# First adaLN vector of a hybrid attention block: its scale part moved to TensorE, its low halves to VectorE, its transfers rebuffered

## The chip, the cores and the metric

The kernel runs on one core of a Trainium2 chip. The metric is the device time of one execution, in microseconds (us). A core has TensorE (PE, whose weight loads are shown apart as PEld), VectorE (DVE), ScalarE (ACT), GpSimd (POOL), and SyncE (SP), whose queue issues the transfers. Each engine works through its own instructions in the order in which they stand; a program orders them when the kernel is built.

## The reference, cut to what matters

```python
ada = (c @ w_ada + b_ada)[:, None, :]            # c: 1 x 1024, w_ada: 1024 x 6144
shift1, scale1, gate1, shift2, scale2, gate2 = jnp.split(ada, 6, axis=-1)
h = rmsnorm(x, g_norm1) * (1.0 + scale1) + shift1     # x: 1024 tokens x 1024
proj = h @ w_in
(q_f, k_f, v_f, f_logit, q_d, k_d, v_d, q_i, k_i, w_i, gate_fox, gate_dsa) = jnp.split(proj, ...)
...
sc = einsum('bqhd,bkd->bqhk', q_idx, k_idx) * idx_scale        # the indexer, 4 heads
iscore = einsum('bqhk,bqh->bqk', relu(sc), w_idx)              # top 256 keys of a query
...
x = x + gate1 * (merged @ w_out)
h2 = rmsnorm(x, g_norm2) * (1.0 + scale2) + shift2
x = x + gate2 * (square(relu(h2 @ w_mlp1)) @ w_mlp2)
return rmsnorm(x, g_final)
```

The change lies in the first two lines for `scale1` and `shift1`, in `h`, and in the loading of the columns of `w_in` for `q_i`, `k_i`, `w_i` and `f_logit`. Two attention branches, the merge and the MLP follow and are not edited.

## The kernel before

The first stage makes `h`, transposed: the 1024 features lie in eight blocks of 128 partitions (index `k`), the tokens along the row in two halves of 512 (index `g`). Products are made in pieces: every operand is split into a high half, rounded to the type fp32r, and a low half, the rest; each product of two such pairs takes three matmuls of 128x512 (`mm3`, hi·hi, lo·hi, hi·lo; all recorded at L75).

Eight tiles `xn` hold x, 128 tokens each; they are normalized in place (L214). The adaLN part goes block by block along `KBS`: blocks 0 and 1 alone, then 2-3, 4-5, 6-7. For each, `load_ada` brings the 1024 rows of `w_ada` for the scale (`j == 1`) and for the shift (`j == 0`) into a tile `wa` (four buffers). In both cases VectorE multiplies the eight row groups by the values of c in `cT` and sums them in `acc` (L245, L247: eight chained instructions), and a matmul with a column of ones sums over the partitions (`ada_cols`, tile `pv`), one column for a block of 128 features. Only for the scale of blocks 0 and 1 TensorE does the sum itself, with the vector c as weights and `wa` streaming. The sums go to `ab` (L175; the scale also L178, L179).

Then TensorE transposes four `xn` pieces into `xT` (two PSUM buffers), ScalarE makes `hf` from it with scale and shift (L267) and the high half `h_hi` (L268), and GpSimd the low half `h_lo` (L270). In the last pair, VectorE does all three for `g == 1`. As soon as a block of `h` is there, the six groups of products of the indexer take it: `S` twice (keys and the small columns), `g` twice, `S` and `tr` (queries), 24 matmuls each. Their weights (`whi`, `wlo`, `qi_w`) are split by ScalarE and GpSimd (L117, L118) from staging tiles `st` (three buffers).

Behind the stage stand, on VectorE, the copies of the indexer's operands (`misc`, `KAi`, `QAi`, `QBi`), and on TensorE first the scores `S<-KAi,QAi` and then the projections `g<-h_hi,whi` of the attention heads. The order on each engine is set when the program is built, by a scheduler that interleaves this code with what follows it; it is therefore different in many places after an edit, and within `tc.high_priority()` the adaLN part goes first.

Of the kernel before, what the change touches and what calls it, by code (L numbers as in the profile page):

```python
# [9 lines left out]
F32 = mybir.dt.float32  # L10
# [47 lines left out]
def block_kernel(ctx: ExitStack, tc: tile.TileContext, x, c, w_ada, b_ada, g_norm1, w_in, b_forget,  # L58
# [15 lines left out]
    def mm(o, l, r, start, stop):  # L74
        nc.tensor.matmul(o, l, r, start=start, stop=stop)  # L75
# [39 lines left out]
    def split_st(st, lo_eng=None, dst=None):  # L115
        hi, lo = dst or [wts.tile([P, 1024], F32R, name=n, tag=n) for n in ("whi", "wlo")]
        nc.scalar.activation(hi, st, AF.Copy)  # L117
        (lo_eng or nc.vector).tensor_tensor(lo, st, hi.bitcast(F32), op=ALU.subtract)  # L118
        return hi, lo
# [58 lines left out]
        nc.vector.tensor_scalar(dst, dst, 1.0, None, op0=ALU.add)  # L178
        nc.vector.tensor_tensor(dst, dst, vecT[:, g0:g0 + n], op=ALU.mult)  # L179

    def misc_weights():
        st = stg.tile([P, 1024], F32, name="st", tag="st")
        sv = st.rearrange("p (k c) -> p k c", k=KT)
        nc.gpsimd.memset(st, 0.0)
        nc.sync.dma_start(sv[:, :, 0:64], win[:, :, C_KI:C_KI + 64])
        nc.sync.dma_start(sv[:, :, 64:72], win[:, :, C_F:C_F + NH])
        nc.sync.dma_start(sv[:, :, 96:100], win[:, :, C_WI:C_WI + NIH])
        return split_st(st, nc.gpsimd)

    wav = w_ada.rearrange("(k p) n -> p k n", p=P)  # L190
    with ExitStack() as st1:
        p1 = pool(st1, "p1")
        sqj = p1.tile([P, D], BF16, name="sqj")
        xn = [p1.tile([P, D], F32, name=f"xn{t}") for t in range(NTT)]
        ss = p1.tile([P, NTT], F32, name="ss")
        nc.scalar.activation(ss[:, 0:1], onesf[:, 0:1], AF.Sqrt)
        def load_x(ts_):
            for t in ts_:
                nc.sync.dma_start(xn[t], xr[t * P:(t + 1) * P, :])

        def load_ada(kt0, n):
            was = []
            for j in (1, 0):
                wt = p1.tile([P, KT, 256], F32, name="wa", tag="wa", bufs=4)[:, :, 0:n * P]
                nc.sync.dma_start(wt, wav[:, :, j * D + kt0 * P:j * D + (kt0 + n) * P])
                was.append((j, wt))
            return was

        def norm_x(g):
            for t in range(4 * g, 4 * g + 4):  # L210
                nc.scalar.activation(sqj, xn[t], AF.Square, accum_out=ss[:, t:t + 1])
            r = newton_rstd(p1, ss[:, 4 * g:4 * g + 4], 4, f"a{g}")
            for t in range(4 * g, 4 * g + 4):
                nc.vector.tensor_scalar(xn[t], xn[t], r[:, t - 4 * g:t - 4 * g + 1], None, op0=ALU.mult)  # L214

        load_x(range(4))
        nc.sync.dma_start(vecs[0:8, :], c.rearrange("o (k p) -> (o k) p", p=P))
        nc.sync.dma_start(vecs[8:16, :], g_norm1.rearrange("(k p) -> k p", p=P))
        nc.sync.dma_start(vecs[16:24, :], g_norm2.rearrange("(k p) -> k p", p=P))
        nc.sync.dma_start(vecs[24:72, :], b_ada.rearrange("(k p) -> k p", p=P))  # L220
        vps = ptr.tile([P, 512], F32, name="vps", tag="tr")
        nc.tensor.transpose(vps[:, 0:P], vecs, ident)
        nc.vector.tensor_copy(vecT, vps[:, 0:P])
        KBS = ((0, 1), (1, 1), (2, 2), (4, 2), (6, 2))
        was = load_ada(*KBS[0])
        load_x(range(4, 8))
        norm_x(0)
        nc.sync.dma_start(bfg[64:64 + NH, :], b_forget.rearrange("(h o) -> h o", o=1))
        first = [misc_weights(), split_w([(0, P, win[:, :, C_QI:C_QI + P])], nc.gpsimd)]
        with tc.high_priority():  # L230
            for kb, (kt0, n) in enumerate(KBS):
                if kb:
                    was = load_ada(kt0, n)
                for j, wt in was:
                    acc = p1.tile([P, 256], F32, name="acc", tag=f"acc{j}")[:, 0:n * P]
                    if j == 1 and kb < 2:
                        ps = ppv.tile([P, 512], F32, name="pv", tag="pv")
                        for k in range(KT):
                            mm(ps[0:1, 0:n * P], cT[:, k:k + 1], wt[:, k, :], k == 0, k == KT - 1)
                        nc.vector.tensor_copy(acc[0:1, :], ps[0:1, 0:n * P])  # L240
                        ada_cols(acc, j, kt0, n, ab[:, 1 - j, :], ppv.tile([P, 512], F32, name="pv", tag="pv"), 1)
                    else:
                        for k in range(KT):
                            if k == 0:
                                nc.vector.tensor_scalar(acc, wt[:, k, :], cT[:, 0:1], None, op0=ALU.mult)  # L245
                            else:
                                nc.vector.scalar_tensor_tensor(acc, wt[:, k, :], cT[:, k:k + 1], acc, op0=ALU.mult, op1=ALU.add)  # L247
                        ada_cols(acc, j, kt0, n, ab[:, 1 - j, :], ppv.tile([P, 512], F32, name="pv", tag="pv"))
                if kb == 0:
                    norm_x(1)  # L250
                if kb == len(KBS) - 1:
                    first.append(split_w([(0, P, win[:, :, C_QI + P:C_QI + 2 * P])], nc.gpsimd,
                                         dst=(qi_w[:, 0:1024], qi_w[:, 1024:2048])))
                norm_scale(ab[:, 0, kt0:kt0 + n], 8 + kt0, n)
                for k in range(kt0, kt0 + n):
                    for g in range(2):
                        gs = slice(g * 512, (g + 1) * 512)
                        ps = ptr.tile([P, 512], F32, name="xT", tag="tr")
                        for t in range(4):
                            nc.tensor.transpose(ps[:, t * P:(t + 1) * P], xn[4 * g + t][:, k * P:(k + 1) * P], ident)  # L260
                        hf = p1.tile([P, 512], F32, name="hf", tag="hf", bufs=4)
                        if kb == len(KBS) - 1 and g == 1:
                            nc.vector.tensor_scalar(hf, ps, ab[:, 0, k:k + 1], ab[:, 1, k:k + 1], op0=ALU.mult, op1=ALU.add)
                            nc.vector.tensor_copy(h_hi[:, k, gs], hf)
                            lo_eng = nc.vector
                        else:
                            nc.scalar.activation(hf, ps, AF.Identity, scale=ab[:, 0, k:k + 1], bias=ab[:, 1, k:k + 1])  # L267
                            nc.scalar.activation(h_hi[:, k, gs], hf, AF.Copy)  # L268
                            lo_eng = nc.gpsimd
                        lo_eng.tensor_tensor(h_lo[:, k, gs], hf, h_hi[:, k, gs].bitcast(F32), op=ALU.subtract)  # L270

    def gemm_h(hi, lo, half, pl=None):
        pl, tag = pl or (pg, "g")
# [929 lines left out]
```

## Time and profile before

| | us |
|---|---|
| median of 3 runs (1656.96 to 1659.05) | 1657.38 |
| the profiled execution's own time | 1664.09 |
| span of the profiled execution | 1662.3 |
| TensorE busy (95% of the span) | 1582.9 |
| VectorE busy (70%) | 1155.4 |
| ScalarE busy (57%) | 955.7 |
| GpSimd busy (41%) | 684.4 |

The profiled execution is 6.7 us above the median, and 1.8 us of its time lie around the span. Busy matmul time counts overlapping pieces, so 95% doesn't mean that TensorE is at its peak.

### The profile page before, as it was taken

The page shows a single profiled execution, that of the slowest core. Times are in us where ns is not written, and L with a number is a line of the kernel's source. Part 1 is how long each engine was busy: PE and PEld are TensorE (multiplying, and loading weights), DVE is VectorE, ACT ScalarE, POOL GpSimd, SP SyncE. Part 2 cuts the span into 40 slices and gives each one's busy share as a digit, 9 for nine tenths or more (in the row PEclk, how much of TensorE's full clock was granted, in tenths as well). Part 3 has the DMA queues.
Part 4 walks back from the last instruction along what each step waited for, and adds up shares of the span by engine and source line. Part 5 has one row for each costly group of instructions (what it writes and reads, how often), then busy time and mean ns, then how long its engine had stood idle before and what let it go on. Part 6 is the DMA issues. An engine that isn't in the chain of part 4 may idle for free.

```text
span 1662.3 us, 22793 instructions
## 1 busy us (share of the span) xinstructions
PE 1582.9 (95%) x7585; PEld 1310.5 (79%) x7585; DVE 1155.4 (70%) x2293; ACT 955.7 (57%) x1674; POOL 684.4 (41%) x569
## 2 busy tenths in 40 slices
PE   5989999998989999999999998999999989999998
PEld 3767787786778888888887787888888868888887
DVE  6786999999954556556666535866565464758987
ACT  4366997898566777677753135554555343533433
POOL 3421121221123574756643211677776544334730
PEclk8999999998999999999999999999999989999999
DMA  9221122222232443444876435554444469665862
GB/s 299 77 59 51 50 74 55 52 66 49 74 77 67 125 133 106 131 143 139 287 257 230 151 121 194 168 185 160 154 147 158 178 240 361 230 212 188 281 209 102
DMA packets 221757, 250.92 MB, mean 151 GB/s; under 512 B 49072, under 2 KB 134144, under 8 KB 221640
## 3 DMA queue, kind: packets, MB, share of 16 engines
q1 hardware_dynamic: 215304, 235.83, 44.8%
q10 hardware_dynamic: 6336, 13.63, 2.1%
q8 instruction: 60, 0.98, 0.2%
q14 instruction: 57, 0.47, 0.1%
HBM read 184.38 MB, written 65.03 MB: 150 GB/s over the span
## 4 chain that ended last, share of the span: by engine, by line
PE 74%; DVE 14%; ACT 4%; DMA 4%; issue 3%; POOL 1%; SPq 1%; DVEq 0%; ACTq 0%; POOLq 0%
PE g L75 33%; PE S L75 23%; PE tr L75 8%; PE pv L75 7%; DVE bjunk L487 3%; PE ptr L572 2%; DVE acc L247 1%; DMA gt<-G_d 1%; DVE pl L574 1%; DVE sp L552 1%; DMA wap<-in_w_ada_dram 1%; ACT eqt L484 1%; ACT sp L556 1%; DVE gt L777 1%; ACT sp L559 1%
## 5 line engine op out<-in xcount | busy, mean ns | idle before, releaser
L75 PE MATMUL g<-h_hi,whi 128*128 128x512 f32 x656 | 266.5, 406 | 8.8 <-DVE KA L314 6.4
L75 PE MATMUL g<-h_hi,wlo 128*128 128x512 f32 x656 | 263.9, 402 | 0.0
L75 PE MATMUL g<-h_lo,whi 128*128 128x512 f32 x656 | 263.0, 401 | 0.0
L118 POOL TENSOR_TENSOR wlo<-st,whi 128x1024 fp32r<-128x1024 f32 x56 | 137.3, 2453 | 293.9 <-ACT whi L117 265.4
L1026 DVE TENSOR_TENSOR ut<-rw,ut 128x1024 fp32r<-128x1024 f32 x112 | 179.0, 1644 | 69.5 <-ACT ut L1025 69.5
L1025 ACT ACTIVATE ut<-rw 128x1024 fp32r<-128x1024 f32 x112 | 112.0, 1052 | 144.9 <-PE pv L75 66.5
L1040 POOL TENSOR_TENSOR rw<-rw 128x1024 f32<-128x1024 f32 x40 | 115.6, 2893 | 127.3 <-DMA rw<-in_w_mlp_dram 110.0
L75 PEld LDWEIGHTS g<-h_hi,whi 128*128 128x128 f32 x656 | 126.2, 192 | 34.8 <-DVE KA L314 4.3
L75 PEld LDWEIGHTS g<-h_hi,wlo 128*128 128x128 f32 x656 | 125.6, 191 | 24.7
L75 PEld LDWEIGHTS g<-h_lo,whi 128*128 128x128 f32 x656 | 125.8, 192 | 23.6
L75 PE MATMUL S<-ut 128*128 128x512 f32 (+1 forms) x576 | 138.2, 384 | 0.0
L75 PEld LDWEIGHTS S<-ut 128*128 128x128 f32 x576 | 106.5, 190 | 21.5 <-DVE ut L1026 0.4
L574 DVE TENSOR_TENSOR pl<-ptr,ph 128x512 fp32r<-128x512 f32 (+1 forms) x160 | 99.5, 630 | 27.2 <-ACT ph L573 23.5
L573 ACT ACTIVATE ph<-ptr 128x512 fp32r<-128x512 f32 (+1 forms) x160 | 86.1, 551 | 55.4 <-PE ptr L572 51.2
L556 ACT ACTIVATE sp<-sp,mn 128x128 f32<-128x128 f32 (+7 forms) x128 | 98.5, 771 | 28.3 <-DVE mn L552 28.1
L117 ACT ACTIVATE whi<-st 128x1024 fp32r<-128x1024 f32 x70 | 73.8, 1054 | 65.9 <-PE g L75 23.1
L487 DVE TENSOR_SCALAR_CACHE_REDUCE bjunk<-sel_all,cand 128x384 bf16<-128x384 int16 (+7 forms) x132 | 106.3, 806 | 1.4
L559 ACT ACTIVATE sp<-sp,mn 128x128 f32<-128x128 f32 (+7 forms) x128 | 96.8, 770 | 17.2 <-DVE mn L558 16.7
L75 PE MATMUL g<-ut 128*128 128x512 f32 (+1 forms) x384 | 94.7, 382 | 6.1 <-ACT ut L1025 4.6
L572 PE MATMUL ptr<-ident,sp 128*128 128x128 f32 x576 | 91.2, 274 | 9.8 <-DVE pl L574 9.8
L75 PE MATMUL pv<-ph,V 128*128 128x256 f32 x320 | 86.8, 291 | 1.6 <-DVE yt L581 0.9
L75 PEld LDWEIGHTS g<-ut 128*128 128x128 f32 x384 | 69.9, 191 | 21.0 <-ACT ut L1025 5.0
(433 smaller groups left out, 3883.4 us busy)
## 6 DMA issues: line engine op xcount, KB each, us to landing
rw<-in_w_mlp_dram SPq DMA_DIRECT2D x72, 512.0 KB
rw<-U_d SPq DMA_DIRECT2D x56, 512.0 KB
wap<-in_w_ada_dram SPq DMA_DIRECT2D x64, 256.0 KB
st<-in_w_mlp_dram SPq DMA_DIRECT2D x32, 512.0 KB
st<-in_w_in_dram SPq DMA_DIRECT2D x26, 512.0 KB
U_d<-cc SPq DMA_DIRECT2D x48, 256.0 KB
st<-in_w_in_dram SPq DMA_DIRECT2D x33, 256.0 KB
G_d<-t SPq DMA_DIRECT2D x32, 256.0 KB
```

Of the source, the lines that this page charges most:

```text
L75: nc.tensor.matmul(o, l, r, start=start, stop=stop)
L117: nc.scalar.activation(hi, st, AF.Copy)
L118: (lo_eng or nc.vector).tensor_tensor(lo, st, hi.bitcast(F32), op=ALU.subtract)
L487: nc.vector.tensor_scalar(bjunk[:, :(i + 1) * P], sel[i].bitcast(dt), thr[:, q], None, op0=ALU.is_ge, op1=ALU.add, accum_out=cnt[:, q])
L556: nc.scalar.activation(sp[:, :W], sp[:, :W], AF.Exp, bias=mn[:, len(cs) - 1:len(cs)], scale=-1.0, accum_out=mn[:, 2:3])
L559: nc.scalar.activation(sp[:, :W], sp[:, :W], AF.Copy, scale=mn[:, 3:4])
L572: nc.tensor.transpose(tr[:, n * P:(n + 1) * P], pt[s][:, kb * P:(kb + 1) * P], ident)
L573: nc.scalar.activation(ph[:, z:], tr[:, z:], AF.Copy)
L574: nc.vector.tensor_tensor(pl[:, z:], tr[:, z:], ph[:, z:].bitcast(F32), op=ALU.subtract)
L1025: nc.scalar.activation(ut[:, n], t, AF.Copy)
L1026: nc.vector.tensor_tensor(ut[:, n + 1], t, ut[:, n].bitcast(F32), op=ALU.subtract)
L1040: nc.gpsimd.tensor_tensor(o, a, b, op=op)
```

## The change

- The scale sums of all blocks go to TensorE, with the 128x128 pieces of `w_ada` as weights and c as the one column that streams: eight matmuls for each block of 128 features, straight into a column of `pv`. VectorE keeps the shift sums. 
- The last pair of `KBS` becomes two single blocks, and the transfers for blocks 6 and 7 go to the staging tiles `st`; `wa` has five buffers, `acc` two.
- The indexer's weights come in one transfer of 324 columns (`wi`) and a small one of 8 (`wf`); ScalarE makes the high and VectorE the low halves, and GpSimd only clears two tiles.
- `h_lo` is made by VectorE everywhere; VectorE makes `hf` and `h_hi` only for the last block's second half.
- The four small vectors are loaded behind the first `xn` tile, no longer behind the fourth.

```diff
         def load_ada(kt0, n):
             was = []
             for j in (1, 0):
-                wt = p1.tile([P, KT, 256], F32, name="wa", tag="wa", bufs=4)[:, :, 0:n * P]
+                if kt0 >= 6:
+                    wt = stg.tile([P, 1024], F32, name="st", tag="st").rearrange("p (k c) -> p k c", k=KT)
+                else:
+                    wt = p1.tile([P, KT, 256], F32, name="wa", tag="wa", bufs=5)[:, :, 0:n * P]
                 nc.sync.dma_start(wt, wav[:, :, j * D + kt0 * P:j * D + (kt0 + n) * P])
                 was.append((j, wt))
             return was
+        wi = p1.tile([P, KT, 324], F32, name="wi")
+        wf = p1.tile([P, KT, NH], F32, name="wf")
+        def idx_weights():
+            nc.sync.dma_start(wi, win[:, :, C_QI:C_QI + 324])
+            nc.sync.dma_start(wf, win[:, :, C_F:C_F + NH])
...
+                for d0, d1, src in ps:
+                    nc.scalar.activation(hv[:, :, d0:d1], src, AF.Copy)
+                    nc.vector.tensor_tensor(lv[:, :, d0:d1], src, hv[:, :, d0:d1].bitcast(F32), op=ALU.subtract)
...
-        KBS = ((0, 1), (1, 1), (2, 2), (4, 2), (6, 2))
+        KBS = ((0, 1), (1, 1), (2, 2), (4, 2), (6, 1), (7, 1))
...
-        first = [misc_weights(), split_w([(0, P, win[:, :, C_QI:C_QI + P])], nc.gpsimd)]
+        first = idx_weights()
...
-                    acc = p1.tile([P, 256], F32, name="acc", tag=f"acc{j}")[:, 0:n * P]
-                    if j == 1 and kb < 2:
+                    if j == 1:
                         ps = ppv.tile([P, 512], F32, name="pv", tag="pv")
-                        for k in range(KT):
-                            mm(ps[0:1, 0:n * P], cT[:, k:k + 1], wt[:, k, :], k == 0, k == KT - 1)
-                        nc.vector.tensor_copy(acc[0:1, :], ps[0:1, 0:n * P])
-                        ada_cols(acc, j, kt0, n, ab[:, 1 - j, :], ppv.tile([P, 512], F32, name="pv", tag="pv"), 1)
+                        for q in range(n):
+                            for k in range(KT):
+                                mm(ps[:, q:q + 1], wt[:, k, q * P:(q + 1) * P], cT[:, k:k + 1], k == 0, k == KT - 1)
+                        nc.vector.tensor_tensor(ab[:, 0, kt0:kt0 + n], ps[:, 0:n], vecT[:, 32 + kt0:32 + kt0 + n], op=ALU.add)
+                        norm_scale(ab[:, 0, kt0:kt0 + n], 8 + kt0, n)
                     else:
+                        acc = p1.tile([P, 256], F32, name="acc", tag="acc", bufs=2)[:, 0:n * P]
...
-                        if kb == len(KBS) - 1 and g == 1:
+                        if k == KT - 1 and g == 1:
...
-                            lo_eng = nc.gpsimd
-                        lo_eng.tensor_tensor(h_lo[:, k, gs], hf, h_hi[:, k, gs].bitcast(F32), op=ALU.subtract)
+                        nc.vector.tensor_tensor(h_lo[:, k, gs], hf, h_hi[:, k, gs].bitcast(F32), op=ALU.subtract)
```

The order moves at three places that matter below. First VectorE, where the shift of blocks 2-3 is summed and turned into `ab`. Before (`acc_318` is this shift, `acc_373` the scale of blocks 4-5, `pv_327` the column sums of the shift):

```order
L247 SCALAR_TENSOR_TENSOR acc_318<-wa_303,vecT_81,acc_318 128x256
L247 SCALAR_TENSOR_TENSOR acc_373<-wa_369,vecT_81,acc_373 128x256
L247 SCALAR_TENSOR_TENSOR acc_318<-wa_303,vecT_81,acc_318 128x256
L247 SCALAR_TENSOR_TENSOR acc_373<-wa_369,vecT_81,acc_373 128x256 x2
L175 TENSOR_TENSOR ab_83<-pv_327,vecT_81 128x2
L245 TENSOR_SCALAR acc_386<-wa_371,vecT_81 128x256
```

After (`acc_322` is the shift of blocks 2-3, `acc_395` that of blocks 4-5, `pv_331` the column sums of the first):

```order
L263 SCALAR_TENSOR_TENSOR acc_322<-wa_300,vecT_81,acc_322 128x256
L261 TENSOR_SCALAR acc_395<-wa_373,vecT_81 128x256
L263 SCALAR_TENSOR_TENSOR acc_395<-wa_373,vecT_81,acc_395 128x256 x7
L175 TENSOR_TENSOR ab_83<-pv_331,vecT_81 128x2
L261 TENSOR_SCALAR acc_460<-st_446,vecT_81 128x128
```

The `ab` that lets blocks 2-3 go now stands behind the whole sum for blocks 4-5, and so behind the landing of `wa_373`. On SP's queue that transfer is the last but one of the adaLN transfers:

```order
L208 DMA wi_134<-in_w_in_dram 128x8x324
L209 DMA wf_135<-in_w_in_dram 128x8x8
L199 DMA wa_298<-in_w_ada_dram 128x8x256
L199 DMA st_444<-in_w_ada_dram 128x8x128
L199 DMA st_446<-in_w_ada_dram 128x8x128
L199 DMA st_490<-in_w_ada_dram 128x8x128
L199 DMA wa_300<-in_w_ada_dram 128x8x256
L199 DMA wa_371<-in_w_ada_dram 128x8x256
L199 DMA wa_373<-in_w_ada_dram 128x8x256
L199 DMA st_492<-in_w_ada_dram 128x8x128
```

The transfers for blocks 6 and 7 have moved ahead of those for the shift of blocks 2-3 and for blocks 4-5. Second, TensorE at the transposes of block 3, where its dense stretch begins. Before:

```order
L75 MATMUL g_623<-h_lo_119,whi_183 128x512
L75 MATMUL g_623<-h_hi_118,wlo_184 128x512
L75 MATMUL pv_327<-onesf_71,acc_318 128x1 x2
L260 MATMUL xT_351<-ident_66,xn0_124 128x128
L260 MATMUL xT_351<-ident_66,xn1_125 128x128
```

After (`pv_375` is the scale of blocks 4-5; a row counts matmuls as written, each is two instructions in the trace):

```order
L75 MATMUL S_683<-h_lo_119,qi_w_110 128x512
L75 MATMUL S_683<-h_hi_118,qi_w_110 128x512
L75 MATMUL pv_331<-onesf_71,acc_322 128x1 x2
L75 MATMUL pv_375<-vecT_81,wa_371 128x1 x13
L272 MATMUL xT_353<-ident_66,xn0_124 128x128
```

Thirteen of the sixteen scale matmuls of blocks 4-5 stand ahead of that transpose. Ahead of it there are, in both programs, 30 matmuls of 128x512 and 24 transposes of the stage; from it to the stage's last product 114 and 40 in both, and 8 matmuls into `pv` before, 23 after (19 for the scale, 4 for the shift). Third, TensorE around the last product of the two groups `S` of the keys, before (`S_562`):

```order
L75 MATMUL S_562<-h_hi_118,wlo_178 128x512
L75 MATMUL g_590<-h_hi_118,wlo_184 128x512
L75 MATMUL g_590<-h_hi_118,whi_183 128x512
L75 MATMUL g_590<-h_lo_119,whi_183 128x512
L75 MATMUL g_590<-h_hi_118,wlo_184 128x512
L75 MATMUL g_623<-h_hi_118,whi_183 128x512
```

and after (`S_589`):

```order
L75 MATMUL S_589<-h_hi_118,wlo_177 128x512
L75 MATMUL g_617<-h_hi_118,whi_178 128x512
L75 MATMUL g_617<-h_lo_119,whi_178 128x512
L75 MATMUL g_617<-h_hi_118,wlo_179 128x512
L75 MATMUL g_650<-h_hi_118,whi_178 128x512
L75 MATMUL g_650<-h_lo_119,whi_178 128x512
```

From there to the last `tr` product 21 matmuls of 128x512 followed before, 13 follow after. Farther up, between the last transposes (`xT`) and the first `tr` product, nine products of `S` and `g` stood before; after, only one column sum into `pv` stands there, and 20 `tr` products follow it at once.

## Rows read from the trace of the kernel before

**Rows 1.** Busy time of each engine by stretch: length, PE, PEld, DVE, ACT, POOL, PEclk, DMA, GB/s.

```profile
25.00:47.80 22.80, 14.73 (x57) 11.29 (x56) 21.35 (x40) 6.61 (x10) 11.36 (x6) 0.70 1.13 311
47.80:70.30 22.50, 21.21 (x108) 17.48 (x108) 19.98 (x34) 9.68 (x17) 11.48 (x8) 0.93 0.20 65
70.30:83.80 13.50, 13.49 (x63) 11.00 (x64) 7.69 (x11) 6.24 (x11) 7.15 (x4) 1.00 0.03 6
87.40:117.00 29.60, 29.60 (x130) 24.21 (x131) 23.44 (x44) 18.86 (x34) 5.96 (x5) 0.94 0.15 31
150.00:500.00 350.00, 324.44 (x1640) 269.18 (x1640) 307.77 (x864) 277.96 (x536) 62.92 (x110) 0.97 0.24 63
```

**Rows 2.** Timeline, DVE and POOL, 24 to 47 us: start, length, instruction, [idle before].

```profile
24.81 5.13 POOL L118 TENSOR_TENSOR wlo<-st,whi 128x1024 fp32r<-128x1024 f32 x2 [2.57 <-ACT whi L117]
25.27 2.45 DVE L247 SCALAR_TENSOR_TENSOR acc<-wa,vecT,acc 128x128 f32<-128x128 f32 x1
...
46.72 0.15 DVE L175 TENSOR_TENSOR ab<-pv,vecT 128x2 f32<-128x2 f32 x1
```

**Rows 3.** Timeline, the start of TensorE's dense stretch.

```profile
46.96 1.45 ACT L267 ACTIVATE hf<-xT,ab 128x512 f32<-128x512 f32 x2 [9.13 <-DVE ab L175]
...
47.79 1.97 PE L260 MATMUL xT<-ident,xn 128*128 128x128 f32 x8 [1.19 <-ACT hf L267]
```

**Rows 4.** Chain that ended last, 40 to 90 us: start, length, what.

```profile
58.09 0.50 DVE acc L247
58.61 0.50 DVE acc L247
...
73.49 3.41 PE tr L75 x15
```

**Rows 5.** Transfers, 0 to 60 us in 40 slices of 1.5 us.

```profile
GB/s 0 224 369 339 358 324 298 319 402 412 406 322 292 270 83 57 328 302 331 347 349 347 350 350 339 354 266 215 285 244 220 361 296 355 255 18 0 0 0 0
```

**Rows 6.** Timeline, eight transposes; four column sums; the `hf` of the last pair.

```profile
58.79 1.03 PEld L260 LDWEIGHTS xT<-ident,xn 128*128 128x128 f32 x8
...
68.46 0.64 PEld L75 LDWEIGHTS pv<-onesf,acc 128*128 128x128 f32 x4
68.68 0.50 PE L75 MATMUL pv<-onesf,acc 128*128 128x1 f32 x4
69.02 0.19 PEld L75 LDWEIGHTS S<-h_lo,whi 128*128 128x128 f32 x1
...
69.48 0.78 ACT L267 ACTIVATE hf<-xT,ab 128x512 f32<-128x512 f32 x1 [6.86 <-DVE ab L175]
```

**Rows 7.** Timeline, from the end of the `S` groups to the first projection.

```profile
78.34 0.62 PE L75 MATMUL S<-h_hi,wlo 128*128 128x512 f32 x2
...
83.37 0.39 PE L75 MATMUL tr<-h_hi,qi_w 128*128 128x512 f32 x1
...
87.38 0.47 PE L75 MATMUL g<-h_hi,whi 128*128 128x512 f32 x1
87.58 0.19 DVE L373 TENSOR_SCALAR wn<-wps 128x32 f32<-128x32 f32 x1
88.24 0.22 DVE L374 COPY xf<-wps 128x64 f32<-128x64 f32 x1
88.38 0.67 DVE L350 TENSOR_TENSOR QBi<-tr,QAi 64x512 fp32r<-64x512 f32 x1
89.08 0.42 DVE L351 CAST QAi<-QAi 64x512 fp32r<-64x512 f32 x1
```

**Rows 8.** Timeline of PE, the first waits of the next stretch.

```profile
118.13 0.50 PE L75 MATMUL S<-KAi,QAi 128*128 128x512 f32 x1 [0.49 <-ACT rl L418]
121.35 0.50 PE L75 MATMUL S<-KAi,QAi 128*128 128x512 f32 x1 [1.56 <-ACT rl L418]
```

**Rows 9.** Groups of DVE instructions, 48 to 72 us: count, busy, mean ns.

```profile
L247 DVE SCALAR_TENSOR_TENSOR acc<-wa,vecT,acc 128x256 f32<-128x256 f32 x22 | 17.9, 836 | 0.4
L270 DVE TENSOR_TENSOR h_lo<-hf,h_hi 128x512 fp32r<-128x512 f32 x1 | 0.7, 692 | 0.0
```

More of the change, by code (lines that the diff above doesn't have):

```diff
@@ L179, in norm_scale @@
         nc.vector.tensor_tensor(dst, dst, vecT[:, g0:g0 + n], op=ALU.mult)
[L181 to L188, printed above, removed]
     wav = w_ada.rearrange("(k p) n -> p k n", p=P)
@@ L207, in load_ada @@
             return was
+        wi = p1.tile([P, KT, 324], F32, name="wi")
[3 more added lines that the diff above has]
+            nc.sync.dma_start(wf, win[:, :, C_F:C_F + NH])
+            whl = [[wts.tile([P, 1024], F32R, name=n, tag=n) for n in ("whi", "wlo")] for _ in range(2)]
+            whl.append((qi_w[:, 0:1024], qi_w[:, 1024:2048]))
+            parts = ([(0, 64, wi[:, :, 256:320]), (64, 72, wf), (96, 100, wi[:, :, 320:324])],
+                     [(0, P, wi[:, :, 0:P])], [(0, P, wi[:, :, P:2 * P])])
+            for n, ((hi, lo), ps) in enumerate(zip(whl, parts)):
+                hv, lv = [t.rearrange("p (k c) -> p k c", k=KT) for t in (hi, lo)]
+                if n == 0:
+                    nc.gpsimd.memset(hi.bitcast(F32), 0.0)
+                    nc.gpsimd.memset(lo.bitcast(F32), 0.0)
+                for d0, d1, src in ps:
+                    nc.scalar.activation(hv[:, :, d0:d1], src, AF.Copy)
+                    nc.vector.tensor_tensor(lv[:, :, d0:d1], src, hv[:, :, d0:d1].bitcast(F32), op=ALU.subtract)
+            return whl
         def norm_x(g):
@@ L214, in norm_x @@
                 nc.vector.tensor_scalar(xn[t], xn[t], r[:, t - 4 * g:t - 4 * g + 1], None, op0=ALU.mult)
-        load_x(range(4))
         nc.sync.dma_start(vecs[0:8, :], c.rearrange("o (k p) -> (o k) p", p=P))
@@ L220, in block_kernel @@
         nc.sync.dma_start(vecs[24:72, :], b_ada.rearrange("(k p) -> k p", p=P))
+        load_x(range(4))
         vps = ptr.tile([P, 512], F32, name="vps", tag="tr")
@@ L250, in block_kernel @@
                     norm_x(1)
[L251 to L254, printed above, removed]
                 for k in range(kt0, kt0 + n):
@@ L261, in block_kernel @@
                         hf = p1.tile([P, 512], F32, name="hf", tag="hf", bufs=4)
-                        if kb == len(KBS) - 1 and g == 1:
+                        if k == KT - 1 and g == 1:
                             nc.vector.tensor_scalar(hf, ps, ab[:, 0, k:k + 1], ab[:, 1, k:k + 1], op0=ALU.mult, op1=ALU.add)
                             nc.vector.tensor_copy(h_hi[:, k, gs], hf)
-                            lo_eng = nc.vector
                         else:
```

## The prediction

> **What bounds the kernel now.** I read the busy time by stretch first. TensorE is busy for 95% of the span, but not in the stage that the change edits: from 25 to 47.8 us it works 14.73 of 22.80 us, at a granted clock of 0.70 on average between its levels of 1.2 and 2.4 GHz, while VectorE works 21.35 [rows 1]. From 47.8 us on this turns: TensorE works 21.21 of 22.50 us and then 13.49 of 13.50. So the stage has two parts with different limits, and what an edit is worth depends on the part.
>
> The first part ends with one event, the `ab` of blocks 2-3: VectorE makes it at 46.72 us [rows 2], ScalarE's `hf` has waited 9.13 us for it and starts at 46.96, and the transposes that need the freed `xT` start at 47.79 [rows 3]. I call this the gate. Before it VectorE's time is long partly because of GpSimd: one sum of 128x128 takes 2.45 us under a GpSimd subtraction of `wlo` [rows 2], and the 22 sums of 128x256 from 48 to 72 us take 836 ns on average [rows 9], where two that follow each other with GpSimd idle start 0.52 us apart [rows 4].
>
> After the gate TensorE decides. Fifteen products take 3.41 us, 0.227 each [rows 4]; eight transposes 1.03, 0.129 each [rows 6]; the loads for the column sums come 0.113 us apart (from 68.68 to 69.02 for three; the first lies beneath the product before) [rows 6]. From the gate to the last `tr` product stand 114 products, 40 transposes and 16 column instructions: 25.9 + 5.2 + 1.8 = 32.9 us. The trace takes from 47.79 to 83.60 (83.37 and one product) [rows 3, 7], 35.8 us; the 2.9 above are waits (1.3 in the first stretch) and a granted clock of 0.93 [rows 1].
>
> **The change, part by part.** *VectorE and GpSimd.* VectorE loses the scale sums of six blocks, 24 instructions of 128x256: 24 x 0.52 = 12.5 us. It gains 14 subtractions `h_lo` of 0.69 us [rows 9], 9.7 us, and the low halves of the weights, whose 2.6 thousand elements on a row are about five times those of an `h_lo`: 3.5 us. So its work stays as it is, but without GpSimd beside it its sums should run at 0.52 and not at 0.84. That gives VectorE some 7 us after the gate [rows 9], where it is not the limit: I cost it at nothing. What hides it is TensorE's dense stretch; if that cover were gone, it would be a gain.
>
> *The gate.* The new order on VectorE puts the `ab` of blocks 2-3 behind the whole shift sum of blocks 4-5, and so behind `wa_373`. Bytes up to its end: x 4.19 MB, 15 of 16 chunks of 8.39 MB, 7.86, the indexer's weights 1.36: 13.41 MB. The trace had moved 11.81 MB at 39.0 us (sum of the slices), and the rest at the 347 GB/s of its middle takes 4.6 us: 43.6 [rows 5]. From that I take 1.6 us: the two slices with 83 and 57 GB/s are the three thin pieces of the indexer's weights, 0.21 MB in 3.0 us, and two of the three are now part of a wide transfer. I add 0.7 us, since three of the first four `xn` now wait behind four small issues (no row prices it; between 0 and a slice of 1.5 us). The landing is then 42.7, eight sums of 0.52 bring 46.9, and `ab` 0.1 more: 47.0, against 46.72 + 0.15 = 46.87 before. The gate stays where it was. Bounds: 1.5 us earlier (all 2.4 us of the thin pieces saved, no late start), 1.6 later (nothing saved, a whole slice late). So the part that was VectorE's becomes the transfers', at the same time.
>
> *Scale on TensorE, ahead of the gate.* 45 of the 64 scale matmuls stand ahead of the gate's transposes, where TensorE is idle for 8 us [rows 1]; hidden. The last 13 of them, 26 instructions, follow the shift sum of blocks 2-3. `wa_300` lands two transfers earlier (2.1 MB, 6.0 us) at 36.7; with one `h_lo`, eight sums and three short ones that sum ends near 42, and 26 x 0.113 = 2.9 us, or 5.9 at half the clock, end between 45 and 48. The gate covers it but for up to 0.4 us.
>
> *Scale on TensorE, behind the gate.* 23 matmuls into `pv` instead of 8, two instructions each: 30 more, 30 x 0.113 = **+3.4 us**. The row is of the same form (128x128 weights, one column), only fewer in a run; the bounds are 0.085 us (0.34 us over four) and 0.19 for a load that nothing covers [rows 6], so 2.6 to 5.7. The Trainium skill ("TensorE: Matmul & The Clock Gate", section "Back-to-back issue gap") gives a gap of about 25 ns for a matmul that streams 1 to 64 columns. By it the 30 would be an estimated 0.75 us and the whole sum below 1.4 us instead of 4.0; but its section "LDWEIGHTS (loading the stationary operand)" charges each load by its columns, some 107 ns for 128, and the row sides with that.
>
> *The end of the stage.* `tr` needs the bank of the last transposes but one, which `hf` must have read. Before, nine products stood between; now 20 `tr` products follow at once behind the last column sum, so TensorE waits for `ab` and `hf`. From the last column sum before (68.68 + 0.37) to the end of that `hf` (69.48 + 0.78) it is 1.2 us [rows 6]: **+1.2**.
>
> So the stage ends at 47.8 + 25.9 + 5.2 + 46 x 0.113 + 1.2 = 85.3 against 83.6, if all 2.9 us of waits and low clock go: +1.7; if none goes, +4.6. I take the first, since `ab` for blocks 4 to 7 now comes early and TensorE has the scale products to fill its waits.
>
> *Behind the stage.* The indexer's copies start from the last product of the two `S`. It stood 21 products before the stage's end and now stands 13 before it: 8 x 0.227 = **+1.8** on top, that is 3.5 us later than the 78.6 of before. From there to the first projection at 87.38 the chain is VectorE's [rows 7]. Its new order puts `wn`, `xf` and the 512-wide `QBi` and `QAi` of `tr` ahead of the cast that the second score product needs: 0.19 + 0.22 + 0.67 + 0.42 = **+1.5** [rows 7]. First projection: +5.0, at 92.4 us.
>
> *After that.* TensorE then has 29.6 us without a gap [rows 1], so the 5.0 stay. The next waits, 0.49 and 1.56 us for `rl` [rows 8], can shrink, because the new order spreads the score products over the projections: between 0 and 2.0 back, I take 1.0.
>
> Sum: 0.1 + 1.7 + 1.8 + 1.5 - 1.0 = **about +4.0 us**, on the profiled execution's own 1664.09 us (span 1662.3 and 1.8 around it): 1668.1. Applied to the median of the runs, 1657.38, it is **1661.4 us**, 0.24% slower. Bounds of this case: gate -1.5, 2.0 back, cheap columns -0.8: +0.6; gate +1.6, none of the 2.9 regained, dear columns +2.3, nothing back: +11.8, of which I hold the upper third unlikely.
>
> **The rivals.** *Transfers come early, no change.* If the wide transfers moved at the best rate of the trace, 412 GB/s, from 21 us on (6.50 MB moved), the other 6.91 MB would land at 37.8, the gate would open 5 us earlier, and the sum would be -0.9: 1656.5. For it: the thin pieces go. Against: the 412 are of 4 KB rows of x, and pieces of `w_ada` moved at 270 to 350 [rows 5]. With the gate 0.7 us earlier than reckoned the whole is within 0.2%, which is what a measurement of this kernel can tell from no change.
>
> *The later order, faster.* The scheduler has moved instructions in attention too. From 150 to 500 us TensorE waits 350 - 324.4 = 25.6 us, with VectorE busy 88% [rows 1]. An order that gave back a third, 8.5 us, would make -4.5: 1652.9. It decides from 4.0 us on, and shows as faster from 7.3. For it: the waits are there, and VectorE is near its limit, where order counts. Against: nothing in the change aims there, no work goes, and the same chance can add waits.
>
> *Low clock after the gate.* The clock was 0.70 ahead of the gate; if one-column products don't raise it and the 2.9 us stay, the time is 1664.3. For it: TensorE idles ahead of the gate still. It differs from the forecast in size only.
>
> **The numbers.** The forecast with its own range (1658 to 1667) I give 0.60, of which 0.15 lies within 0.2%; low clock 0.08; early transfers 0.10; the later order 0.22. So faster by over 0.2%: 0.22; within: 0.25; slower: 0.53. The range over all, 1652 to 1667, leaves out the rest of the later order and the dear columns.
>
> **What will show it.** Right: the `ab` of blocks 2-3 at 47 us with VectorE waiting for `wa` before it, not for GpSimd; no GpSimd subtraction from 5 to 75 us; TensorE without gaps from 48 us on with 46 `pv` instructions, then one gap of a microsecond ahead of `tr`; the last `S` product near 82, the first projection near 92; and from there the same distance to the end. Wrong: the gate at 43 or earlier; the scale products at well under 0.1 us; or a distance from the first projection to the end that differs by over 3 us.

## The result, and the profile after

The changed kernel takes 1667.87 us (median of 4 runs, 1666.64 to 1669.71), the kernel before beside it 1658.22 (1656.96 to 1659.57): a ratio of 1.0059, with a 95% interval of 1.0041 to 1.0077. It is slower, as forecast, but by 9.7 us and not by 4.0, and lies 0.9 us above the range.

First the busy time by stretch of the kernel after (columns as in [rows 1]); the second part cuts the start of the stage finer.

```profile
25.00:47.80 22.80, 16.16 (x84) 13.03 (x82) 14.63 (x38) 6.57 (x11) 0.00 (x0) 0.98 0.86 251
47.80:70.30 22.50, 21.95 (x111) 20.03 (x112) 9.90 (x31) 8.86 (x14) 0.00 (x0) 0.72 0.11 28
70.30:83.80 13.50, 13.31 (x78) 11.40 (x76) 3.37 (x9) 3.94 (x7) 0.00 (x0) 1.00 0.33 72
...
42.50:48.30 5.80, 0.58 (x6) 0.46 (x4) 3.82 (x10) 0.00 (x0) 0.00 (x0) 0.86 0.03 11
48.30:54.00 5.70, 5.65 (x27) 5.65 (x28) 3.68 (x10) 2.48 (x4) 0.00 (x0) 0.50 0.10 26
54.00:60.00 6.00, 6.00 (x23) 5.32 (x23) 1.60 (x5) 2.59 (x4) 0.00 (x0) 0.50 0.21 63
60.00:66.00 6.00, 6.00 (x34) 5.06 (x33) 0.25 (x2) 0.06 (x1) 0.00 (x0) 0.97 0.00 0
```

The 0.98 of the first row is no gain on the 0.70 of [rows 1]: up to 32.6 us TensorE's 128x512 products start 0.43 us apart, the pace of half clock, and from 33 us on 0.23. The record of this profile shows no clock before 33 us, and the row counts that time as full.

GpSimd does nothing here, and VectorE has half of its work from [rows 1] left in the second stretch (9.90 us for 19.98). But TensorE's clock there is 0.72, where it was 0.93; and from 48.3 to 60 us it is 0.50, the lower of its two levels, although TensorE is busy for 11.65 of 11.70 us. Just ahead of that it idles for 5.2 us.

The timeline of the same kernel, VectorE ahead of the gate and TensorE from there on (start, length, instruction, idle before), shows why. It answers to [rows 2], [rows 3] and [rows 7].

```profile
44.23 0.35 DVE L261 TENSOR_SCALAR acc<-wa,vecT 128x256 f32<-128x256 f32 x1 [2.00 <-DMA wa<-in_w_ada_dram]
44.62 3.61 DVE L263 SCALAR_TENSOR_TENSOR acc<-wa,vecT,acc 128x256 f32<-128x256 f32 x7
48.15 0.15 DVE L175 TENSOR_TENSOR ab<-pv,vecT 128x2 f32<-128x2 f32 x1
...
42.58 0.50 PE L75 MATMUL pv<-onesf,acc 128*128 128x1 f32 x4
48.35 5.71 PE L75 MATMUL pv<-vecT,wa 128*128 128x1 f32 x26 [5.27 <-DVE ab L175]
53.92 1.09 PE L272 MATMUL xT<-ident,xn 128*128 128x128 f32 x4
...
55.84 0.78 PE L75 MATMUL S<-h_hi,whi 128*128 128x512 f32 x1
...
66.63 1.84 PE L75 MATMUL pv<-vecT,st 128*128 128x1 f32 x16
...
84.67 0.50 PE L75 MATMUL tr<-h_hi,qi_w 128*128 128x512 f32 x1 [1.06 <-ACT hf L278]
...
90.25 0.62 PE L75 MATMUL S<-h_hi,wlo 128*128 128x512 f32 x2
...
93.44 0.39 PE L75 MATMUL tr<-h_hi,qi_w 128*128 128x512 f32 x1
...
96.65 0.41 PE L75 MATMUL S<-KAi,QAi 128*128 128x384 f32 x1 [1.85 <-DVE QAi L361]
100.07 0.69 PE L75 MATMUL S<-KAi,QBi 128*128 128x384 f32 x1 [3.01 <-DVE QBi L362]
100.62 0.76 PE L75 MATMUL g<-h_hi,whi 128*128 128x512 f32 x1
```

From 42.58 to 43.1 us TensorE writes the shift sums of blocks 2-3 into `pv`. The next in its order are the scale products of blocks 4-5. They write to the same pool, which has one buffer, so they wait until `ab` has read it, and VectorE makes that `ab` only behind the next shift sum (48.15). Then 26 instructions run at half clock, 0.22 us each, and the transposes that the gate had set free come behind them, at 53.92 instead of 47.79. The first projection is 13.2 us late.

### The profile page after: what moved, and what is told of

Read it like the earlier page. It is cut to its first block, busy times and chain, and to the rows that moved or that the text cites. A ratio compares the mean times of both kernels' runs of the same rounds, so it can differ in the third digit from the quotient of the medians.

```text
span 1664.9 us, 22960 instructions
## 1 busy us (share of the span) xinstructions
PE 1585.1 (95%) x7665; PEld 1320.4 (79%) x7665; DVE 1140.5 (69%) x2296; ACT 956.6 (57%) x1678; POOL 658.3 (40%) x553
## 4 chain that ended last, share of the span: by engine, by line
PE 73%; DVE 13%; ACT 4%; DMA 4%; issue 4%; POOL 1%; SPq 1%; ACTq 0%; DVEq 0%; POOLq 0%
PE g L75 31%; PE S L75 23%; PE tr L75 8%; PE pv L75 8%; DVE bjunk L497 3%; PE ptr L582 2%; DVE sp L562 1%; DVE pl L584 1%; DMA wa<-in_w_ada_dram 1%; ACT eqt L494 1%; DMA wap<-in_w_ada_dram 1%; ACT sp L566 0%; DMA wi<-in_w_in_dram 0%; ACT sp L569 0%; DMA M_d<-t 0%
## 5 line engine op out<-in xcount | busy, mean ns | idle before, releaser
L118 POOL TENSOR_TENSOR wlo<-st,whi 128x1024 fp32r<-128x1024 f32 x54 | 131.8, 2441 | 388.0 <-ACT whi L117 269.1
L75 PE MATMUL pv<-pl,V 128*128 128x256 f32 x320 | 84.0, 289 | 3.2 <-DVE pl L584 2.8
```

## The experiments

The table gives, from the profiled execution of each kernel (us), the end of the last `tr` product, the start of the first projection, and the time from attention's first `pv` to the first product with `isc`. Beside it stand the median with its count, and the ratio to runs of the kernel before on the same chip. Their medians differ from chip to chip (1658.2 to 1661.1), so where a microsecond matters the ratio decides.

| kernel | `tr` ends | projection | `pv` to `isc` | median | ratio, 95% |
|---|---|---|---|---|---|
| before, again (e8) | 83.5 | 87.13 | 523.3 | 1658.62 (1) | |
| after | 93.8 | 100.62 | 517.0 | 1667.87 (4) | 1.0059, 1.0041 to 1.0077 |
| e1 | 95.9 | 102.73 | 515.6 | 1665.93 (6) | 1.0046, 1.0031 to 1.0061 |
| e2 | 83.0 | 90.75 | 514.6 | 1657.32 (12) | 0.9993, 0.9983 to 1.0002 |
| e3 | 95.0 | 99.30 | 515.1 | 1665.17 (6) | 1.0036, 1.0022 to 1.0050 |
| e4 | 84.7 | 89.67 | 519.5 | 1659.17 (12) | 0.9993, 0.9981 to 1.0005 |
| e5 | 90.2 | 94.91 | 518.6 | 1663.51 (10) | 1.0025, 1.0008 to 1.0042 |
| e6 | 87.8 | 95.46 | 515.6 | 1666.64 (10) | 1.0044, 1.0028 to 1.0060 |
| e7 | 86.1 | 93.25 | 523.6 | 1663.62 (10) | 1.0029, 1.0015 to 1.0043 |
| e9 | 90.7 | 95.40 | 514.1 | 1661.74 (10) | 1.0019, 1.0010 to 1.0028 |
| e10 | 82.3 | 85.94 | 523.5 | 1658.83 (12) | 1.0001, 0.9988 to 1.0013 |
| e11 | 83.8 | 87.37 | 524.0 | 1659.07 (12) | 1.0001, 0.9988 to 1.0014 |
| e12 | 83.0 | 87.99 | 515.6 | 1654.72 (12) | 0.9968, 0.9956 to 0.9981 |

**e8, the kernel before once more.** No edit.

> The kernel before, unchanged, for a second profile: the first profiled execution took 1664.1 us against a median of 1657.4. If the distance lies in the stage of the change, the first projection stands elsewhere than at 87.4 us; if it lies behind, the stage is the same within 0.5 us and the difference of 3 to 6 us is found between 150 and 1650 us.

The stage is the same within 0.3 us (87.13 for 87.38), and the 5.5 us that its span is shorter (1656.8 for 1662.3) lie behind it. So the first profile of before shows the stage well but is 5 us long later; behind the stage I compare with this one. The 5 us lie between the first projection and attention's first `pv` (87.3 us and 85.3) and behind the first product with `isc` (964.2 and 961.1); from `pv` to `isc` the two profiles agree (523.4 and 523.3). So a difference of 2 to 3 us in the first and the last of these stretches is no more than two profiles of one kernel show.

### The parts of the change, one by one

**e3, scale on TensorE alone.** The kernel before with this at the head of the chunk's loop:

```diff
-                    if j == 1 and kb < 2:
-                        ... (c as the weights, then a row)
+                    if j == 1:
+                        for q in range(n):
+                            for k in range(KT):
+                                mm(ps[:, q:q + 1], wt[:, k, q * P:(q + 1) * P], cT[:, k:k + 1], k == 0, k == KT - 1)
```

> The kernel before with one part of the change: the scale sums of all blocks on TensorE, one column at a time; transfers, chunk buffers and GpSimd's low halves as before. Theory A (the bank and the half clock): 26 column instructions stand at the gate again, the first `xT` behind it comes 5 to 6 us behind `ab`, the time is 1663 to 1670. Theory B (the transfers and the order cost it): VectorE has 12.5 us less to do ahead of the gate and beside GpSimd, the gate opens 1 to 3 us earlier, and the time is 1654 to 1659. Theory C (the extra column instructions alone, 30 at 0.113): 1660 to 1662.

Theory A: this part alone makes 5.9 us of the time. The timeline and the stretches of e3:

```profile
52.48 3.06 PE L75 MATMUL pv<-vecT,wa 128*128 128x1 f32 x26 [0.25 <-DVE ab L175]
55.40 0.63 PE L260 MATMUL xT<-ident,xn 128*128 128x128 f32 x4
```

```profile
48.30:54.00 5.70, 5.45 (x32) 4.66 (x30) 3.10 (x8) 1.48 (x3) 0.00 (x0) 1.00 0.76 250
54.00:60.00 6.00, 6.00 (x34) 5.52 (x35) 1.21 (x3) 3.71 (x6) 4.79 (x4) 0.66 0.00 0
60.00:66.00 6.00, 6.00 (x26) 4.84 (x25) 2.48 (x6) 0.00 (x0) 0.26 (x1) 0.77 0.00 0
```

Here the 26 instructions follow wide products with a gap of 0.25 us only and run at full clock, 0.118 us each, and still the clock falls behind them, while TensorE is busy throughout.

**e4, `h_lo` on VectorE alone.** The kernel before with `lo_eng = nc.vector` for all.

> The kernel before with one part of the change: the 14 subtractions `h_lo` on VectorE instead of GpSimd. Theory A (VectorE isn't the limit behind the gate; its sums run at 0.52 us without GpSimd beside them): within 2 us of the kernel before, either side. Theory C (VectorE's load costs the time): 14 times 0.69 us are 9.7 us on an engine that was busy 20 of 22.5 us, and the time is 1660 or more. If VectorE's sums are what the stage waits for, and they go from 0.84 to 0.52 us, the time falls by 2 or more.

No change in the time, as Theory A says. The profile has a loss and a gain in it: the first projection is 2.5 us later, and the time from `pv` to `isc` is 3.8 us shorter.

**e7, the transfers alone.** The kernel before with the load order, the buffers, the single blocks 6 and 7 and the indexer's weights of the change.

> The kernel before with the transfers of the change alone: chunks in five buffers and the staging tiles, small vectors first, the indexer's weights as one transfer with their low halves on VectorE; scale sums and `h_lo` on VectorE and GpSimd as before. Theory A (only scale on TensorE costs): within 2 us of the kernel before. Theory B (later transfers and new order): 2 to 8 us slower, with a gate at 48 or later.

4.5 us slower, against Theory A, though not by Theory B's gate: `ab` opens it at 44.35. What is late comes afterwards. The timeline of e7:

```profile
45.08 8.28 DVE L262 SCALAR_TENSOR_TENSOR acc<-wa,vecT,acc 128x256 f32<-128x256 f32 x10
...
58.65 2.65 DVE L262 SCALAR_TENSOR_TENSOR acc<-st,vecT,acc 128x128 f32<-128x128 f32 x2
...
64.12 0.59 PE L75 MATMUL pv<-onesf,acc 128*128 128x1 f32 x2 [2.36 <-DVE acc L262]
```

```profile
47.80:70.30 22.50, 20.14 (x90) 16.49 (x89) 20.04 (x45) 9.20 (x16) 12.09 (x10) 0.80 0.30 71
```

Ten sums take 8.28 us, 0.83 each, with GpSimd's `h_lo` beside them (12.09 us of work from 47.8 to 70.3). Later two instructions of 128x128 take 2.65 us, and TensorE waits 2.36 us for a sum made in that time. So the contention of [rows 9] is still there, and is waited for in the stage, which ends 2.6 us later. The granted clock has a part in that: it was 0.80 in this stretch and 0.93 before [rows 1], by estimate 2.9 us of 22.5, and no scale product of this kernel stands there on TensorE. How the loss divides between the two isn't shown. Another 3.5 us are lost from the end of the stage to the first projection.

**e2, the change without scale on TensorE.** All scale sums as in the kernel before (blocks 0 and 1 too, with c as the weights), the rest as in the change.

> The changed kernel with the scale sums of blocks 2 to 7 back on VectorE (8 multiply-adds and a short sum over columns each, as in the kernel before); transfers, staging tiles and the low halves of h on VectorE as in the change. Theory A (scale on TensorE costs the time, by the bank, the half clock and the extra instructions): no 26 column instructions at the gate, the clock behind it at 0.9 again, and the time at or below the kernel before, 1654 to 1660. Theory B (the transfers' later end and the new order cost it): the gate at 48 or later, the time 1663 to 1668. Theory C (VectorE is short of time with 24 more sums of 0.52 us, 12.5 us, and the low halves): the gate moves to 50 or later, the time over 1668.

1657.32: within 0.2% of the kernel before, and 10.5 us below the changed kernel. The gate opens at 44.28. Transfers and `h_lo` together cost nothing, though the transfers without `h_lo` on VectorE cost 4.5 us (e7): with GpSimd idle a sum takes 0.41 to 0.50 us (0.83 in e7). What is left of the change is scale on TensorE, and taking it out gives back all of the loss.

### Where the scale products stand, and the clock

**e1, one `pv` tile with columns of its own for each pair.**

```diff
+        pvs = ppv.tile([P, 512], F32, name="pv", tag="pv")
-                        ps = ppv.tile([P, 512], F32, name="pv", tag="pv")
+                        ps = pvs[:, 16 * kb:16 * kb + n]
```

> The changed kernel with one edit: all column sums of the vector stand in one tile `pv` with columns of their own, so that the scale products of the next blocks needn't wait until `ab` has read the bank. Their place in TensorE's order is unchanged (26 instructions ahead of the transposes of block 3). Theory A (the bank holds the scale products back until the gate opens): they run before the gate, the first `xT` behind it starts at 48 to 49 instead of 53.9 us, the clock after it is nearer to 0.9, and the time falls by 4 to 7 us, to 1661-1664. Theory B (the added column instructions cost their time wherever they stand): they still run, only elsewhere, the time stays within 2 us of 1667.9. Theory C (the order after the stage costs it): the stage ends earlier but the first projection doesn't; within 2 us of 1667.9.

The edit did not free the products. The timeline of e1:

```profile
51.25 4.94 PE L75 MATMUL pv<-vecT,wa 128*128 128x1 f32 x26 [3.49 <-DVE ab L175]
56.05 1.09 PE L273 MATMUL xT<-ident,xn 128*128 128x128 f32 x4
```

They still wait for the `ab` that reads other columns of the bank (at 51.04, since the chunk ahead of it landed 2.9 us later than in the changed kernel). The Trainium skill ("PSUM — Partial Sum Buffer", section "Terms") says that TensorE's write and another engine's access must not meet in one bank and the same partitions at once. The Trainium skill ("Perfetto Trace Analysis", section "Matmuls") advises that independent groups rotate through different banks. The trace shows that this program waits, 3.49 us in one bank; that the chip would demand it no run here shows, and the wait may as well come from how the program keeps track of a tile. A bank of their own wasn't tried: the program's pools hold 2 + 3 + 2 + 1 tiles of a bank each, eight, as many as the first of these two pages counts. So e1 tells nothing between A and B. What it adds is one more pair of times: the products start 0.2 us behind that `ab` in four kernels, wherever it stands (48.15 and 48.35 in the changed kernel, 51.04 and 51.25 here, 52.27 and 52.48 in e3, 44.54 and 44.76 in e6).

**e5, scale products ahead of the shift sums in the program**, so that `pv` passes to them earlier:

```diff
+            scale_cols(0, was[0][1])
             for kb, (kt0, n) in enumerate(KBS):
+                j, wt = was[1]
+                if kb + 1 < len(KBS):
+                    was = load_ada(*KBS[kb + 1])
+                    scale_cols(kb + 1, was[0][1])
```

> The changed kernel with the scale columns of the next blocks put ahead of the shift sums of the blocks before them in the program, so that the one `pv` bank passes to them earlier: TensorE's order now has the 32 column instructions of blocks 4-5 some 25 rows ahead of the gate and 16 of block 6 at the gate. Theory A (26 column instructions at the gate, behind the bank, cost 6 us): only 16 are left there, the first `xT` of block 3 starts at most 3.6 us behind `ab` (5.7 before), and the time falls by 2 to 6 us from 1667.9. Theory B (the added column work costs the same wherever it stands): 1666 to 1669. If the scale chunks' transfers hold the earlier transposes up, the gate comes later and the time is above 1668.

Theory A: 4.4 us back (5.6 by the ratios), first projection at 94.91. The timeline of e5 shows 30 of the 32 of blocks 4-5 well ahead of the gate (its `ab` comes at 53.37), and 16 of block 6 at it:

```profile
42.11 4.39 PE L75 MATMUL pv<-vecT,wa 128*128 128x1 f32 x30 [1.02 <-DMA wa<-in_w_ada_dram]
...
53.75 1.84 PE L75 MATMUL pv<-vecT,st 128*128 128x1 f32 x16
55.45 1.07 PE L275 MATMUL xT<-ident,xn 128*128 128x128 f32 x8
```

**e6, c as the weights, the chunk streaming.**

```diff
-                                mm(ps[:, q:q + 1], wt[:, k, q * P:(q + 1) * P], cT[:, k:k + 1], k == 0, k == KT - 1)
+                            mm(ps[0:1, 0:n * P], cT[:, k:k + 1], wt[:, k, :], k == 0, k == KT - 1)
```

> The changed kernel with the scale sums of all blocks still on TensorE and in the same places, but with c as the one-column weights and the chunk streaming (8 products of 256 columns for two blocks, and two short column products to turn the row), instead of 16 products of one column behind a load of 128 columns each. Theory A' (what costs is the time of one-column products and the low clock that they leave, 0.72 from 48 to 70 us): the products at the gate take 2 to 4 us instead of 5.7, the clock behind them is nearer to 0.9, and the time falls by 3 to 6 us, to 1662-1665. Theory A (any scale work there, because of the bank): the wait of 5 us ahead of it stays, and the time falls by at most 2 us. The way over a row, a copy and two more passes through the bank can cost 1 to 2 us at each pair of blocks; then it stays at 1667 or more.

The timeline and a stretch of e6:

```profile
44.76 3.61 PE L75 MATMUL pv<-wa,vecT 128*1 128x256 f32 x16 [0.25 <-DVE ab L175]
48.30 1.09 PE L273 MATMUL xT<-ident,xn 128*128 128x128 f32 x8
```

```profile
48.30:54.00 5.70, 5.70 (x34) 4.83 (x34) 4.78 (x13) 2.49 (x4) 0.00 (x0) 1.00 0.00 0
```

Here the products wait 0.25 us and not 5.27, since VectorE's new order has `ab` (44.54) ahead of the next sum. The clock is as A' expects: as long a run of products, behind the same gap of 0.25 us, but streaming 256 columns each, leaves it at 1.00, where e3's fell to 0.66. It is one pair of profiles. The first projection is 5.2 us earlier than after. But the time falls by 1.2 us only (2.5 by the ratios, whose intervals overlap), which A' did not expect: in the profiles 3.0 us of it are lost again between the first projection and the first `pv` (89.1 us for 86.1) and 3.4 behind the first `isc` (1664.8 - 700.1 = 964.7 for 961.3). That is as much as the two profiles of before differ by there, so one profile can't say whether it is lost at all.

**e9, both of these edits.**

> The changed kernel with both edits on its scale sums: put ahead of the shift sums in the program, and with c as the weights and the chunk streaming. Its order of attention comes out as in the kernel before. Theory A with A' (what costs in the stage is where the scale products stand and the clock they leave): the first projection falls to 89-93 us, from 100.6, 94.9 and 95.5. Theory D: the 5 us that the later order had given back are gone, so the time is 1661 to 1665 in spite of that. Theory E: the earlier stage shows in the time, 1655 to 1660.

1661.74, the lowest with the scale on TensorE, though not clear of e5 by the ratios, but the first projection is at 95.40 and not at 89 to 93: the two gains don't add up. And Theory D's place is wrong: this kernel's late part has the order of before (from `isc` on), yet its time from `pv` to `isc` is the short one.

### What is given back later

**e10 and e11: the kernel before with some of the `h_lo` on VectorE**, those of blocks 0 and 1 (`k < 2`) and those of the right halves (`g == 1`).

> The kernel before with one small edit: the subtractions `h_lo` of blocks 0 and 1 on VectorE, those of blocks 2 to 7 on GpSimd as before. The stage's row count up to the two `KAi` products and up to attention is that of the kernel before, but the scheduler's order of attention comes out as in the changed kernel (the `g` products with `Yd` ahead of the last `S` ones). Theory D (the later order gives 4 to 6 us back, from the first attention product to the products of `big` 832 instead of 837 us): the first projection at 86 to 89 us and the time 1653 to 1656, faster than both. Theory E (the time behind the stage shrinks only because a late stage leaves less to wait for): with the stage on time nothing is given back, and the time is within 2 us of the kernel before.

> As the run before, but it is the subtractions `h_lo` of the right half of every block that are on VectorE and those of the left half on GpSimd: another edit that leaves the stage's row count and gives the later order of the changed kernel. Theory D: 1653 to 1656 with the first projection at 86 to 89 us; if the halves on VectorE delay its sums, the first projection is at 90 or later and the time near that of the kernel before. Theory E: within 2 us of the kernel before.

Both are at the kernel before, 0.01% from it with an interval of 0.14% at most: Theory D as stated is wrong. The products of `Yd` come in the other order, and that gives nothing. Yet the table speaks against E too: e7 is late and has 523.6 us from `pv` to `isc`, e4 is nearly on time and has 519.5. The times fall into two groups, 514 to 520 and 523 to 524, and the groups are those of the scheduler's order at the start of attention: 83 or 87 matmuls between its first `S` and its first `pv`.

**e12: `h_lo` of blocks 6 and 7 alone on VectorE**, which leaves TensorE's order as before up to the last transposes and gives the order with 83 matmuls.

```diff
-                            lo_eng = nc.gpsimd
+                            lo_eng = nc.vector if k >= 6 else nc.gpsimd
```

> The kernel before with the subtractions `h_lo` of blocks 6 and 7 on VectorE, the others on GpSimd as before. TensorE's order is that of the kernel before up to the last transposes; the order of attention comes out as in the changed kernel, with two score products of the indexer and 83 rows, instead of 87, between the first `S` of attention and the first `pv`. Theory D' (what is given back stands between the first `pv` of attention and the first product with `isc`, 514 to 519 us in this order and 523.5 in the other, whatever the stage took): 514 to 520 us there, the first projection at 86 to 90, and the time 1651 to 1657, faster than the kernel before by 0.1 to 0.5%. Theory E (what is given back comes from the late stage): 523 us there and the time within 2 us of the kernel before.

Theory D': 515.6 us there, the first projection at 87.99, and a kernel that is faster than both: 0.32% below the kernel before (1654.72 against 1661.08 beside it), and by the ratios 0.91% below the changed one. TensorE's waits between `pv` and `isc` (line, waited for, us in total, times, longest) of e8, and then of e12:

```profile
PE ptr L572 <- DVE pl L574: 8.6, 3, 4.1
PE S L75 <- DVE mn L552: 6.1, 8, 1.1
PE g L75 <- DVE KA L314: 5.6, 4, 2.2
PE pv L75 <- DVE pl L574: 1.4, 2, 0.9
PE pv L75 <- DVE yt L581: 0.9, 1, 0.9
PE pv L75 <- ACT ph L573: 0.7, 2, 0.5
```

```profile
PE g L75 <- DVE KA L314: 5.7, 4, 2.8
PE ptr L572 <- DVE pl L574: 3.5, 2, 3.4
PE pv L75 <- DVE yt L581: 3.5, 2, 2.3
PE pv L75 <- ACT ph L573: 3.2, 3, 2.4
PE pv L75 <- DVE pl L574: 2.9, 3, 1.1
PE S L75 <- DVE mn L552: 2.1, 5, 0.9
PE ptr L572 <- DVE nct L480: 0.6, 1, 0.6
PE g L75 <- ACT t L598: 0.5, 1, 0.5
PE pv L75 <- DVE mn L558: 0.3, 1, 0.3
```

The waits of `ptr` for `pl` and of `S` for `mn` fall by 9.1 us and others grow by 8.1: in all 22.3 us for 23.3. Most of the 7.8 us stands in TensorE's busy time, 6.1 us. The same stretch of e8 and of e12, by engines:

```profile
172.45:695.77 523.32, 499.23 (x2603) 419.97 (x2602) 405.38 (x1114) 400.73 (x779) 167.11 (x228) 0.98 0.30 82
```

```profile
175.82:691.38 515.56, 493.12 (x2602) 417.20 (x2601) 399.50 (x1113) 400.36 (x777) 166.02 (x228) 0.99 0.30 82
```

And of e7 (87 matmuls) and e4 (83):

```profile
179.70:703.30 523.60, 501.69 (x2603) 424.15 (x2602) 403.39 (x1114) 400.20 (x779) 168.81 (x228) 0.97 0.30 81
177.20:696.70 519.50, 497.45 (x2601) 421.07 (x2600) 402.03 (x1113) 400.99 (x777) 165.96 (x228) 0.98 0.30 81
```

The granted clock is not the same in them, though the two decimals hide it. Unrounded, one less the clock, times the stretch, is 10.2 us in e8, 6.8 in e12, 15.4 in e7 and 12.0 in e4. By this estimate 3.4 of the 7.8 us between e8 and e12 go with the clock. With it taken out 513.1, 508.7, 508.2 and 507.6 us are left, and the two groups no longer stand apart. So the time goes with the order in every profile of the table, and e12's was said beforehand; how much of it the order makes by its waits, how much comes by the clock, and which of the moved products matter is not shown.

## Where the prediction was right, and where it failed

Right were the direction, GpSimd's being without work from 25 to 83.8 us, and the terms below. VectorE had 10.1 us less to do in the second stretch, where some 7 had been reckoned, at no price either way.

- *The price of a column instruction.* 16 in 1.84 us, 0.115 each, for 0.113 (at half clock it is 0.22). The Trainium skill's gap for few columns ("TensorE: Matmul & The Clock Gate", "Back-to-back issue gap") would be an estimated 0.025; its "LDWEIGHTS (loading the stationary operand)", 107 ns for 128 columns, agrees with the trace at full clock.
- *The end of the stage.* `tr` waits 1.06 us for `hf`, forecast 1.2.
- *Behind the stage.* From the last `tr` to the first projection it is 100.62 - 93.83 = 6.8 us, against 87.38 - 83.76 = 3.6 [rows 7]: 3.2 longer, forecast 1.8 + 1.5.

The step that failed is *Scale on TensorE, ahead of the gate*: "The gate covers it but for up to 0.4 us." I had read when the chunk lands and what stands ahead of the products, but not that their `pv` comes from a pool of one buffer, and that the `ab` which frees it is the gate itself. So they could not start before the gate, and stood in front of all that the gate sets free. Against the rows of before the first projection's 13.2 us are:

- the gate, 48.15 for 46.72: +1.4 (forecast +0.1, bound 1.6), since the chunk was there at 44.2 and not 42.7;
- the 26 instructions behind it: 53.92 - 47.79 - 1.4 = +4.7 (forecast at most 0.4);
- from there to the last `tr`: 93.83 - 53.92 = 39.9 us for 36.0, +3.9 (forecast +1.7). The 46 column instructions that I had put there are all there. The 2.2 more go with the low clock, which I had taken as regained: six microseconds at 0.50, of which half is lost. As a rival of its own, *low clock after the gate*, it had 0.08;
- +3.2 behind it, as above.

That scale on TensorE is the cost is shown from both sides: +5.9 us alone (e3) and -10.5 when it is taken out (e2). The two are not the same size: with the rest of the change TensorE idles 5.27 us ahead of the 26 instructions and runs them in 5.71, in e3 it idles 0.25 and takes 3.06; what else is in the difference is open. That some half of the cost goes with where the products stand is shown by e5 (-4.4 us, with the clock at 1.00 from 54 to 60 us). How much of that is the clock is not shown: e6 kept it at 1.00, but VectorE's order and the gate (44.54) moved with it, and its time hardly fell. That the products wait for the `ab` is shown by four kernels, in which they start 0.2 us behind it. e1 was to show that the bank holds them back, and failed; a `pv` of their own is untested.

*After that* was mis-sized the other way: 1.0 back was forecast, and it is 5.4 against e8 (first projection 13.5 us later, span 8.1 longer), over the 3 us that the prediction had named as a sign of being wrong. These are single profiles; by the medians, 9.7 us for the 13.2 of the first projection, it is 3.5. The rival *the later order* came in part: 6.3 us between `pv` and `isc`, where it spoke of 8.5, but on top of the loss in the stage and not in its place.

## What to carry to other kernels

Work that "fills the idle time ahead of a wait" does so only if its own buffers are free before that wait: look up who frees them, in the pool's count, and ask what stands behind it in the engine's order. Before giving TensorE one-column sums, look at the clock behind them along with their own time. And where a scheduler orders a whole program, a small edit can move the order far behind it, and the time can change there more than where it stands: with one condition (e12) the kernel was 0.3% faster, the whole change cost 0.6%.

## What was not expected of the hardware

One-column products, with a load of 128 columns each, need not hold the clock up: in e3 it fell to 0.66 behind 26 of them that followed wide products with a gap of 0.25 us, and after the 26 at the gate it took until about 60 us, some 4 us of mostly wide products, to rise again. It does not always fall: behind 32 of them in 3.63 us at 34.65 us the changed kernel's clock was 1.00 from 36 to 42.5 us.
